# Every second unit of an up-projection by seven products of quarters, in a one-core float32 decoder layer

## Chip, cores and metric

One Trainium2 chip, one of its cores. The metric is the device time of one execution in microseconds (us); lower is better.

## What is computed

One step of a hybrid decoder layer on 2048 prompt rows and 32 sample rows, width 1024, all in float32. The part that the change touches is the channel mixer behind the first layer norm:

```python
def conv_glu_ffn(x, conv_state, w_up, conv_w, conv_b, w_down):      # x: rows x 1024
    L = x.shape[1]
    a, g = jnp.split(x @ w_up, 2, axis=-1)                          # w_up: 1024 x 5632
    ext = jnp.concatenate([conv_state.astype(a.dtype), a], axis=1)
    conv = conv_b
    for j in range(CONV_W):                                         # 3 taps
        conv = conv + ext[:, j:j + L] * conv_w[j]
    h = jax.nn.gelu(conv) * g
    return h @ w_down, ext[:, -(CONV_W - 1):]                       # w_down: 2816 x 1024
```

Before it stand the input projection, a state-space branch, window attention and their merge; behind it a residual sum and a second layer norm.

## The kernel before

The 2048 prompt rows are taken in four blocks of 512; the 32 sample rows ride with the second block, whose tiles are 544 columns wide and whose products run as 256 and 288 columns. In a block the stages follow one another: input projection, state-space branch and attention beside the gates, merge, first layer norm, up-projection and down-projection.

**A product of float32 matrices is three.** Each operand is split into a high and a low part (`x1h`, `x1l` of the activations, `wh`, `wl` of the weights), and high by high, high by low and low by high are summed in PSUM (`ws_unit`, the matmuls of L262). A weight tile `wr` (128 x 1024, six buffers) comes by DMA from the SP queue; `split_to` (L220) makes `wh` on ACT by a copy and `wl` on DVE by a subtraction, or on POOL (`G`) when the tile's place in the program's list `order` leaves 2 on division by 3. `wh` and `wl` have four buffers each. `W.get(key)` takes the next tile of the list, issues loads up to three tiles further on and splits up to two tiles further on; `W.ahead()` does one more split. So a weight is split in program order among the other work of ACT and DVE, a little ahead of its matmuls.

**A unit of the up-projection** is 128 of the 2816 hidden channels: tile `ua` gives the convolution's half, `ug` the gate's half, each 24 matmuls of 512 columns (8 slices of 128 input channels, 3 products). `ffn_tail` then works on one tile after another: ACT copies PSUM to `ae`, ACT makes the first tap `cv`, DVE adds two taps, ACT squares into `cq`, DVE multiplies, ACT takes the tanh, DVE finishes the gelu; `ffn_gate` multiplies by the gate from PSUM on DVE, and `split` makes `hh` on ACT and `hl` on DVE for the down-projection. The split of a weight stands between the taps and the gelu (`meanwhile`).

**Groups.** The 22 units stand in two groups of 12 and 10 (`GROUPS`). Behind each group comes its part of the down-projection: two halves `h` of 512 output columns, `nu` weight tiles `dn` in each, 24 matmuls of 512 columns a tile; `dn_evict` adds the result to the rows `z` (tiles `xr`) on DVE.

The program is not reordered: the instructions of each engine stand in the order in which the code writes them, and `bg.tick()` (one per half unit or `dn` tile) is where background steps of other stages are written in: the layer norm's scaling of the rows on POOL (`x1_rows`), the transposes of the next block's input (`x_split`) and so on.

## Time and profile before

| | |
|---|---|
| median of 3 runs | 2846.28 us (2841.29 to 2846.91) |
| profiled execution | 2843.99 us |
| its span, first to last instruction | 2842.2 us |
| PE (matmuls) busy | 2811.4 us, 99% of the span, 15180 matmuls |
| PEld (weight loads) busy | 2392.7 us, 84% |
| DVE, ACT, POOL busy | 1698.5 us (60%), 1162.1 us (41%), 1005.9 us (35%) |
| DMA | 304.25 MB, mean 107 GB/s |
| mean granted TensorE clock | 0.997 of 2.4 GHz |

The profiled execution lies 2.3 us under the median; 1.8 us of it lie outside the span. PE is TensorE's matmuls and PEld its weight loads, which overlap them; DVE is VectorE, ACT ScalarE, POOL GpSimd, SP the engine that issues most DMAs. A busy PE is not a PE at its peak, since the records of successive matmuls overlap.

### The profile page before, as it was taken

How to read it: one execution, taken by the hardware profiler on the slowest of the kernel's cores; microseconds unless marked ns; L12 is line 12 of the kernel's file. 1: busy time of each engine (PE TensorE's matmuls, PEld its weight loads, DVE VectorE, ACT ScalarE, POOL GpSimd, SP SyncE). 2: the span in 40 equal slices, each digit the busy share in tenths (PEclk: the TensorE clock that was granted, in tenths of full speed). 3: DMA queues.
4: the chain of work that ended last, by engine and by line, in shares of the span. 5: the costliest groups of instructions: out<-in, count | busy, mean ns of one | idle time of the engine just before them, and what ended most of it. 6: DMA issues, size and time to landing. Idle time of an engine off the chain costs nothing.

```text
span 2842.2 us, 39299 instructions
## 1 busy us (share of the span) xinstructions
PE 2811.4 (99%) x15180; PEld 2392.7 (84%) x15180; DVE 1698.5 (60%) x2673; ACT 1162.1 (41%) x2039; POOL 1005.9 (35%) x1070
## 2 busy tenths in 40 slices
PE   9999999999999999999999999999999999999998
PEld 8887888888999989989978878888888887888887
DVE  6984676254586467634647735762545854674355
ACT  4535354243335426423424442542433453344241
POOL 1764244121445413512207731351124661252122
PEclk9999999999999999999999999999999999999999
DMA  5423233334622432223345324223245433233232
GB/s 155 154 78 119 81 90 105 93 97 135 180 71 70 132 107 80 89 69 106 106 119 180 99 79 134 82 97 104 87 136 155 118 101 126 82 97 111 82 98 76
DMA packets 414494, 304.25 MB, mean 107 GB/s; under 512 B 51147, under 2 KB 350498, under 8 KB 414290
## 3 DMA queue, kind: packets, MB, share of 16 engines
q1 hardware_dynamic: 411490, 293.77, 34.5%
q0 software_dynamic: 2816, 7.96, 0.8%
q8 instruction: 119, 1.95, 0.3%
q14 instruction: 69, 0.57, 0.1%
HBM read 285.30 MB, written 17.39 MB: 106 GB/s over the span
## 4 chain that ended last, share of the span: by engine, by line
PE 91%; DVE 4%; POOL 2%; issue 1%; ACT 1%; DMA 0%; DVEq 0%; POOLq 0%; SPq 0%; ACTq 0%
PE ps L262 58%; PE ps L266 9%; PE ps L268 8%; PE ps L267 8%; PE ps L318 3%; PE ps L989 1%; POOL m L121 1%; PE ps L799 1%; DVE wl L121 1%; DVE t L121 1%; PE ps L274 1%; DVE m L121 0%; POOL ht L121 0%; PE ps L939 0%; DVE scr L121 0%
## 5 line engine op out<-in xcount | busy, mean ns | idle before, releaser
L121 POOL TENSOR_TENSOR wl<-wr,wh 128x1024 fp32r<-128x1024 f32 x136 | 338.0, 2485 | 899.0 <-ACT wh L113 806.6
L113 ACT ACTIVATE wh<-wr 128x1024 fp32r<-128x1024 f32 (+1 forms) x449 | 470.3, 1050 | 261.0 <-PE ps L268 250.2
L262 PE MATMUL ps<-x1l,wh 128*128 128x512 f32 (+2 forms) x1856 | 569.1, 342 | 0.0
L262 PE MATMUL ps<-x1h,wl 128*128 128x512 f32 (+2 forms) x1856 | 567.6, 341 | 0.0
L262 PE MATMUL ps<-x1h,wh 128*128 128x512 f32 (+2 forms) x1856 | 567.5, 341 | 0.0
L121 DVE TENSOR_TENSOR wl<-wr,wh 128x1024 fp32r<-128x1024 f32 (+1 forms) x313 | 407.8, 1306 | 201.1 <-ACT wh L113 199.9
L262 PEld LDWEIGHTS ps<-x1h,wh 128*128 128x128 f32 x1856 | 325.5, 188 | 42.9 <-issue 0.8
L262 PEld LDWEIGHTS ps<-x1l,wh 128*128 128x128 f32 x1856 | 325.7, 188 | 42.1 <-DVE x1l L121 0.3
L262 PEld LDWEIGHTS ps<-x1h,wl 128*128 128x128 f32 x1856 | 325.6, 188 | 41.0
L262 PE MATMUL ps<-xh,wh 128*128 128x512 f32 (+1 forms) x880 | 285.8, 357 | 5.5 <-ACT yk L113 1.4
L262 PE MATMUL ps<-xh,wl 128*128 128x512 f32 (+1 forms) x880 | 281.0, 352 | 5.1 <-POOL wl L121 2.5
L118 DVE SCALAR_TENSOR_TENSOR cv<-ae,pc,cv 128x512 f32<-128x512 f32 x176 | 145.4, 826 | 227.1 <-ACT cv L115 224.0
L262 PE MATMUL ps<-xl,wh 128*128 128x512 f32 (+1 forms) x880 | 280.5, 351 | 0.0
L266 PE MATMUL ps<-wh,hh 128*128 128x512 f32 x704 | 279.9, 398 | 0.0
L268 PE MATMUL ps<-wh,hl 128*128 128x512 f32 x704 | 277.9, 395 | 0.0
L267 PE MATMUL ps<-wl,hh 128*128 128x512 f32 x704 | 277.0, 394 | 0.0
L1654 POOL COPY cc<-ae 128x2 f32<-128x2 f32 x88 | 19.6, 223 | 492.2 <-ACT ae L113 491.4
L262 PEld LDWEIGHTS ps<-xh,wh 128*128 128x128 f32 x880 | 156.2, 189 | 30.2 <-issue 2.4
L262 PEld LDWEIGHTS ps<-xh,wl 128*128 128x128 f32 x880 | 156.3, 189 | 29.7 <-DVE wl L121 3.9
L262 PEld LDWEIGHTS ps<-xl,wh 128*128 128x128 f32 x880 | 156.7, 189 | 20.3
L266 PEld LDWEIGHTS ps<-wh,hh 128*128 128x128 f32 x704 | 132.6, 188 | 34.6 <-issue 5.0
L268 PEld LDWEIGHTS ps<-wh,hl 128*128 128x128 f32 x704 | 132.2, 188 | 30.9
(357 smaller groups left out, 4889.6 us busy)
## 6 DMA issues: line engine op xcount, KB each, us to landing
wr<-in_w_up SPq DMA_DIRECT2D x176, 512.0 KB
wr<-in_w_down SPq DMA_DIRECT2D x88, 512.0 KB
wr<-in_w_in SPq DMA_DIRECT2D x87, 512.0 KB
wr<-in_w_glu SPq DMA_DIRECT2D x64, 256.0 KB
wr<-in_w_o SPq DMA_DIRECT2D x32, 512.0 KB
wr<-in_w_in SPq DMA_DIRECT2D x34, 256.0 KB
xin<-in_x_prompt SPq DMA_DIRECT2D x32, 256.0 KB
wr<-in_w_attn_br SPq DMA_DIRECT2D x32, 256.0 KB
```

The lines of the kernel that those rows point to most:

```text
L113: A.activation(out, in_, AF.Copy, scale=scale, **kw)
L118: eng.scalar_tensor_tensor(out, a, s, b, op0=op0, op1=op1, **kw)
L121: eng.tensor_tensor(out, a, b, op=op)
L262: T.matmul(ps[:, :n], w[:, k, :], x[k][:, c0:c0 + n], start=(i == 0), stop=(i == len(ops) - 1))
L266: T.matmul(ps[:m], ah, wh, start=first, stop=False)
L267: T.matmul(ps[:m], ah, wl, start=False, stop=False)
L268: T.matmul(ps[:m], al, wh, start=False, stop=last)
L274: T.matmul(ps[r:r + 32], a, w, start=(k < 4), stop=(k >= n - 4))
L318: T.transpose(out, in_, ident[:k, :k])
L799: T.matmul(xv[:, a, r, :], C.t[n][:, a_ * 128:(a_ + 1) * 128], C.uv[:, a_, :], start=True, stop=True)
L989: T.matmul(B.ops[qb][r, :], vt[:, qb + kt, r], pt[kt], start=(kt == 0), stop=(kt == 1))
L1654: G.tensor_copy(cc[:, :, f], ae[:, 512:514])
```

## The change

For two square halves of rows and of channels, a product of 2 x 2 quarters can be made of seven products of sums of quarters in place of eight. The change takes the tokens of a block in two halves (`hn` = 256, or 272 in the second block) and the 1024 input channels in two halves; the two column halves are a unit's `a` and `g`. In blocks two to four, every second unit from unit 6 on (`F0`; units 6, 8, ..., 20) is made in this way by `seven(f)`: 7 products of 4 slices x 3 = 12 matmuls of `hn` columns, 84 in place of 48 of 512. The following odd unit stays as it was, and `two_units` writes both together, in the order `sc` (products 1 and 5), `sa` (2 and 6), `sb` (3 and 7), `ua` of the odd unit, `sd` (product 4), `ug` of the odd unit.

- **Sums of weights** are made once, in block one: `weight_sums`, one of three steps at each tick, loads four quarters of w_up (256 KB each), makes four sums on DVE, splits two of them, and writes 1.5 MB to DRAM; 8 times. Later `sc` and `sa` load a quarter and a sum (256 KB each) into a `wr` tile and split it on ACT and DVE, never on POOL; `sb` loads its high and low parts (512 KB each) straight into `wh` and `wl`; `sd` is half a tile.
- **Sums of activations** are made per block by `x1_sums` (12 background steps on DVE and ACT in the first group and its down-projection), from the whole-precision copies `x1f`, which now stay until then.
- **The results** are put together by `seven`: ACT copies products 1 and 5 to `us`; DVE adds 2 and 6, then 3 and 7, into `ae`, then runs the same taps and gelu, and makes the gate's half in `gt`.
- **Groups** are now four, of 6, 6, 4 and 6 units, The up-projection meets the down-projection four times a block, and the rows `z` are added to twice as often. `x1_rows` and `x_split` stand at closer ticks. In the last group of the last block all three `dn` tiles of the second half are held and run tile by tile (before: the last four of five). One small instruction in the very last layer norm goes from POOL to DVE.

The diff, cut to its core:

```diff
-GROUPS = ((0, 12), (12, 22))
+GROUPS = ((0, 6), (6, 12), (12, 16), (16, 22))
+LG = len(GROUPS) - 1
+F0 = 6
...
+    def weight_sums():
...
+                    t[i, j] = S("ws")
+                    SP.dma_start(k4(t[i, j][:, 0:512]), quarter(f, i, j))
+            yield
+            tt(t[1, 1], t[1, 0], t[1, 1], OP.add)
+            tt(t[1, 0], t[0, 0], t[1, 0], OP.subtract)
+            tt(t[0, 0], t[1, 1], t[0, 0], OP.subtract)
+            tt(t[0, 1], t[0, 1], t[0, 0], OP.subtract)
+            yield
+            hi = [S("wsh", dt=F32R) for _ in range(2)]
+            lo = [S("wsl", dt=F32R) for _ in range(2)]
+            for h, l, s in zip(hi, lo, (t[0, 1], t[1, 0])):
+                act(h, s)
+                tt(l, s, h.bitcast(F32), OP.subtract)
+            def out(f=f, s1=t[1, 1], s2=t[0, 0], hi=hi, lo=lo):
+                SP.dma_start(sums["s1", f], s1)
+                SP.dma_start(sums["s2", f], s2)
+                for n, x in (("hi", hi), ("lo", lo)):
+                    for i in range(2):
+                        SP.dma_start(sums[n, f][:, i * 512:(i + 1) * 512], x[i].bitcast(F32))
+            bg.add(1, out)
+            del t, hi, lo, out
+            yield
...
+        if k == "sa":
+            return lambda t: [(k4(t[:, 0:512]), quarter(key[1], 0, 1)), (t[:, 512:1024], sums["s2", key[1]])]
+        if k == "sc":
+            return lambda t: [(k4(t[:, 0:512]), quarter(key[1], 0, 0)), (t[:, 512:1024], sums["s1", key[1]])]
+        if k == "sd":
+            return lambda t: [(k4(t[:, 0:512]), quarter(key[1], 1, 1))]
...
+            dn = [("dn", g, h, i) for h in range(2) for i in range((f1 - f0) // 2)]
+            if b and f0 >= F0:
+                for f in range(f0, f1, 2):
+                    order += [("sc", f), ("sa", f), ("sb", f), ("ua", f + 1), ("sd", f), ("ug", f + 1)]
+                order += dn
+            else:
+                for f in range(f0, f1):
+                    order += [("ua", f), ("ug", f)]
+                order += dn
...
+                key = order[self.dmas]
+                if key[0] == "sb":
+                    two = [wp.tile([128, 1024], F32R, name=uid(n_), tag=n_, bufs=4) for n_ in ("wh", "wl")]
+                    for t, n_ in zip(two, ("hi", "lo")):
+                        SP.dma_start(t.bitcast(F32), sums[n_, key[1]])
+                    self.ready[self.dmas] = tuple(two)
+                    self.dmas += 1
+                    continue
...
         def split_to(self, n, eng=None):
             while self.splits < min(n, len(order)):
+                if self.splits in self.ready:
+                    self.splits += 1
+                    continue
                 t = self.raw.pop(self.splits)
+                c = 512 if order[self.splits][0] == "sd" else 1024
                 hi = wp.tile([128, 1024], F32R, name=uid("wh"), tag="wh", bufs=4)
                 lo = wp.tile([128, 1024], F32R, name=uid("wl"), tag="wl", bufs=4)
-                act(hi, t)
-                e = eng or (G if self.splits % 3 == 2 and self.splits > 24 and order[self.splits][0] != "u" else V)
-                tt(lo, t, hi.bitcast(F32), OP.subtract, eng=e)
+                act(hi[:, 0:c], t[:, 0:c])
+                e = eng or (G if self.splits % 3 == 2 and self.splits > 24
+                            and order[self.splits][0] not in ("u", "sa", "sc", "sd") else V)
+                tt(lo[:, 0:c], t[:, 0:c], hi[:, 0:c].bitcast(F32), OP.subtract, eng=e)
...
-            bg.add(6 + 3 * i, lambda i=i: x1_rows(i))
...
+        def x1_sums():
+            lo_, hi_ = slice(0, hn), slice(hn, n)
+            for k in range(4):
+                t12, t34 = S("t12", 544), S("t34", 544)
+                tt(t12[:, lo_], x1f[k][:, hi_], x1f[k][:, lo_], OP.subtract)
+                tt(t12[:, hi_], x1f[k + 4][:, hi_], t12[:, lo_], OP.subtract)
+                yield
+                tt(t34[:, lo_], x1f[k + 4][:, hi_], x1f[k][:, hi_], OP.subtract)
+                tt(t34[:, hi_], x1f[k + 4][:, lo_], t12[:, hi_], OP.subtract)
+                del x1f[k], x1f[k + 4]
+                th[0, k], tl[0, k] = split(B, t12, None, "t")
+                yield
+                th[1, k], tl[1, k] = split(B, t34, None, "t")
+                del t12, t34
+                yield
+        if B.b:
+            x1s = x1_sums()
+            for i in range(12):
+                bg.add(5 + i, lambda: next(x1s, None))
...
                 act(ae[:, 2 + c0:2 + c0 + c], pa[i][:, 0:c])
+            conv(f, ae, pa[1][:, 256:288] if B.sp else None)
+            meanwhile()
...
+        def product(o, w, part, x):
+            hi, lo = (k4(t[:, part * 512:part * 512 + 512]) for t in w)
+            ws_unit(hi, lo, 4, *x, [(0, hn)], [o])
...
+            w = W.get(("sc", f))
+            _, p1, p5 = banks()
+            product(p1, w, 0, quarters(0, 0))
+            product(p5, w, 1, row_sums(1))
+            u, gt, ae = S("us", 544), S("gt", 544), S("ae", 546)
+            G.tensor_copy(ae[:, 0:2], cc[:, :, f])
+            act(u[:, 0:hn], p1)
+            act(u[:, hn:n], p5)
+            del p1, p5, _
+            yield
+            w = W.get(("sa", f))
+            both, p2, p6 = banks()
+            product(p2, w, 0, quarters(1, 0))
+            product(p6, w, 1, row_sums(2))
+            add(ae[:, 2:2 + n], u[:, 0:hn], both, p2, p6)
+            del both, p2, p6
+            yield
+            w = W.get(("sb", f))
+            _, p3, p7 = banks()
+            product(p3, w, 0, quarters(1, 1))
+            product(p7, w, 1, row_sums(3))
+            c12 = ae[:, 2 + hn:2 + n]
+            tt(u[:, 0:hn], c12, p7, OP.add)
+            tt(c12, c12, p3, OP.add)
+            tt(c12, c12, u[:, hn:n], OP.add)
+            del p3, p7, _
+            conv(f, ae, ae[:, 514:546])
+            c_ = fst.c
+            del ae, c12
             q = S("cq", 544)
             act(q[:, 0:n], c_[:, 0:n], AF.Square)
+            yield
             stt(q[:, 0:n], q[:, 0:n], 1.0 / GELU_A, c_[:, 0:n], OP.add, OP.mult)
             act(q[:, 0:n], q[:, 0:n], AF.Tanh, scale=GELU_S * GELU_A)
+            yield
+            p4 = P()[:, 0:hn]
+            product(p4, W.get(("sd", f)), 0, row_sums(4))
             stt(c_[:, 0:n], q[:, 0:n], 1.0, c_[:, 0:n], OP.add, OP.mult)
-            fst.c = c_
+            tt(gt[:, hn:n], u[:, 0:hn], u[:, hn:n], OP.add)
+            tt(gt[:, 0:hn], u[:, 0:hn], p4, OP.add)
+            del p4
+            stt(c_[:, 0:n], c_[:, 0:n], 0.5, gt[:, 0:n], OP.mult, OP.mult)
+            hh[f], hl[f] = split(B, c_, None, "h", hs.get(f))
+            yield
+        def two_units(f):
+            t = seven(f)
+            next(t)
+            next(t)
+            bg.tick()
+            next(t)
+            w = [x.rearrange("p (k m) -> p k m", k=8) for x in W.get(("ua", f + 1))]
+            pa = ws_unit(*w, 8, x1h, x1l, cols)
+            next(t)
+            bg.tick()
+            next(t)
+            bg.tick()
+            ffn_tail(f + 1, pa, lambda: None)
+            w = [x.rearrange("p (k m) -> p k m", k=8) for x in W.get(("ug", f + 1))]
+            pg = ws_unit(*w, 8, x1h, x1l, cols)
+            hh[f + 1], hl[f + 1] = ffn_gate(f + 1, pg, W.ahead)
+            bg.tick()
...
+                if B.b == 0:
+                    bg.steps = weight_sums()
+            quartered = B.b and f0 >= F0
+            for f in range(f0, f1, 2) if quartered else ():
+                two_units(f)
+            for f in () if quartered else range(f0 or 2, f1):
...
-                        bg.add(2 + k, lambda k=k: x_split(nxt, k))
+                        bg.add(2 + k // 2, lambda k=k: x_split(nxt, k))
```

On DVE, in the third block's second group of units, the program before has, for one unit f and the start of the next (`ps` is PSUM, `xr` the rows, the other names are those above):

```order
L121 TENSOR_TENSOR hl_18771<-cv_18723,hh_18770 128x512
L118 SCALAR_TENSOR_TENSOR cv_18803<-ae_18799,pc,cv_18803 128x512 x2
L121 TENSOR_TENSOR wl_18810<-wr_18764,wh_18809 128x1024
L118 SCALAR_TENSOR_TENSOR cq_18813<-cq_18813,cv_18803 128x512
L118 SCALAR_TENSOR_TENSOR cv_18803<-cq_18813,cv_18803 128x512
L118 SCALAR_TENSOR_TENSOR cv_18803<-cv_18803,ps_18818 128x512
L121 TENSOR_TENSOR hl_18851<-cv_18803,hh_18850 128x512
```

The change has, on DVE in the same block, for units 6 and 7, from the split of unit 8's `sc` to behind the split of unit 8's `sa` (`wl_18379` and `wl_18420`):

```order
L126 TENSOR_TENSOR wl_18379<-wr_18340,wh_18378 128x1024
L123 SCALAR_TENSOR_TENSOR cv_18334<-cq_18338,cv_18334 128x512
L126 TENSOR_TENSOR gt_18262<-us_18261 128x256
L126 TENSOR_TENSOR gt_18262<-us_18261,ps_18374 128x256
L123 SCALAR_TENSOR_TENSOR cv_18334<-cv_18334,gt_18262 128x512
L126 TENSOR_TENSOR hl_18399<-cv_18334,hh_18398 128x512
L123 SCALAR_TENSOR_TENSOR cv_18406<-ae_18402,pc,cv_18406 128x512 x2
L123 SCALAR_TENSOR_TENSOR cq_18410<-cq_18410,cv_18406 128x512
L123 SCALAR_TENSOR_TENSOR cv_18406<-cq_18410,cv_18406 128x512
L126 TENSOR_TENSOR wl_18420<-wr_18375,wh_18419 128x1024
L123 SCALAR_TENSOR_TENSOR cv_18406<-cv_18406,ps_18423 128x512
L126 TENSOR_TENSOR hl_18452<-cv_18406,hh_18451 128x512
```

Before, one unit's taps and gelu stand between two splits; now the end of unit 6 and the taps and gelu of unit 7 stand between the splits of `sc` and `sa`.

On ACT, before, for one unit of that group:

```order
L113 ACTIVATE hh_18770<-cv_18723 128x512
L113 ACTIVATE ae_18799<-ps_18774 128x512
L115 ACTIVATE cv_18803<-ae_18799,pc 128x512
L113 ACTIVATE wh_18809<-wr_18764 128x1024
L115 ACTIVATE cq_18813<-cv_18803 128x512
L115 ACTIVATE cq_18813<-cq_18813 128x512
L113 ACTIVATE wh_18846<-wr_18807 128x1024
L113 ACTIVATE hh_18850<-cv_18803 128x512
```

With the change, on ACT, for units 6 and 7, from unit 6's first tap to unit 7's `hh` (`wh_18343` is unit 7's `ug`, `wh_18378` unit 8's `sc`, `wh_18419` unit 8's `sa`):

```order
L120 ACTIVATE cv_18334<-ae_18263,pc 128x512
L120 ACTIVATE cq_18338<-cv_18334 128x512
L118 ACTIVATE wh_18343<-wr_18299 128x1024
L120 ACTIVATE cq_18338<-cq_18338 128x512
L118 ACTIVATE wh_18378<-wr_18340 128x1024
L118 ACTIVATE hh_18398<-cv_18334 128x512
L118 ACTIVATE ae_18402<-ps_18347 128x512
L120 ACTIVATE cv_18406<-ae_18402,pc 128x512
L120 ACTIVATE cq_18410<-cv_18406 128x512
L120 ACTIVATE cq_18410<-cq_18410 128x512
L118 ACTIVATE wh_18419<-wr_18375 128x1024
L118 ACTIVATE hh_18451<-cv_18406 128x512
```

Unit 7's copy out of PSUM, `ae_18402`, now stands behind unit 6's last step, `hh_18398`, and the split of unit 8's `sa` behind unit 7's tanh.

## Rows read from the trace of the kernel before

**Rows 1.** The page: the chain that ended last, shares of the span by engine.

```profile
PE 91%; DVE 4%; POOL 2%; issue 1%; ACT 1%; DMA 0%; DVEq 0%; POOLq 0%; SPq 0%; ACTq 0%
```

**Rows 2.** Waits, engine PE: who was waited for; us in total, times, longest.

```profile
PE ps L858 <- POOL ht L121: 3.0, 1, 3.0
PE ps L262 <- POOL wl L121: 2.5, 1, 2.5
```

**Rows 3.** Windows: us, busy us (xinstructions) of PE, PEld, DVE, ACT, POOL, PEclk, DMA, GB/s.

```profile
2000.00:2100.00 100.00, 100.00 (x434) 81.20 (x433) 58.48 (x67) 47.00 (x64) 21.12 (x23) 1.00 0.37 118
...
1300.00:1420.00 120.00, 120.00 (x960) 120.00 (x959) 72.73 (x102) 56.79 (x106) 29.74 (x46) 1.00 0.34 106
```

**Rows 4.** Timeline, PE: start us, us, instruction; 256-column matmuls, 45 rows with both ends.

```profile
1797.92 0.28 PE L262 MATMUL ps<-x1h,wl 128*128 128x256 f32 x1
...
1803.15 0.28 PE L262 MATMUL ps<-x1l,wh 128*128 128x256 f32 x1
```

**Rows 5.** Lines by form, DVE, 1992 to 2103: xcount | busy us, mean ns | idle before.

```profile
L121 DVE TENSOR_TENSOR wl<-wr,wh 128x1024 fp32r<-128x1024 f32 x13 | 15.9, 1220 | 0.0
L118 DVE SCALAR_TENSOR_TENSOR cv<-ae,pc,cv 128x512 f32<-128x512 f32 x20 | 15.0, 752 | 36.6 <-ACT cv L115 36.2
...
L118 DVE SCALAR_TENSOR_TENSOR cv<-cq,cv 128x512 f32<-128x512 f32 x9 | 6.2, 693 | 6.3 <-ACT cq L115 6.3
```

**Rows 6.** Lines by form, ACT, 1992 to 2103.

```profile
L113 ACT ACTIVATE wh<-wr 128x1024 fp32r<-128x1024 f32 x19 | 19.9, 1045 | 0.0
L115 ACT ACTIVATE cv<-ae,pc 128x512 f32<-128x512 f32 x10 | 8.2, 816 | 0.9
L115 ACT ACTIVATE cq<-cv 128x512 f32<-128x512 f32 x10 | 6.3, 633 | 6.6 <-DVE cv L118 6.6
L113 ACT ACTIVATE ae<-ps 128x512 f32<-128x512 f32 x10 | 6.0, 600 | 37.8 <-PE ps L262 37.8
```

**Rows 7.** Lines by form, DVE, whole span: adds of 256 columns from PSUM.

```profile
L121 DVE TENSOR_TENSOR m<-ps,tber 128x256 f32<-128x256 f32 x16 | 6.7, 417 | 0.1
```

**Rows 8.** Timeline, 2008 to 2021: one unit's chain on ACT and DVE, beside POOL.

```profile
2009.42 0.60 ACT L113 ACTIVATE ae<-ps 128x512 f32<-128x512 f32 x1 [3.43 <-PE ps L262]
...
2011.96 2.81 POOL L121 TENSOR_TENSOR wl<-wr,wh 128x1024 fp32r<-128x1024 f32 x1 [1.62 <-ACT wh L113]
...
2013.20 2.12 DVE L118 SCALAR_TENSOR_TENSOR cq<-cq,cv 128x512 f32<-128x512 f32 x1 [0.70 <-ACT cq L115]
...
2016.02 0.69 DVE L118 SCALAR_TENSOR_TENSOR cv<-cq,cv 128x512 f32<-128x512 f32 x1 [0.70 <-ACT cq L115]
...
2020.53 0.60 ACT L113 ACTIVATE ae<-ps 128x512 f32<-128x512 f32 x1 [2.36 <-PE ps L262]
```

**Rows 9.** Timeline, PE: the longest wait.

```profile
184.93 0.49 PE L858 MATMUL ps<-cw,ht 128*128 128x128 f32 x2 [2.98 <-POOL ht L121]
```

**Rows 10.** Windows behind and around waits of PE.

```profile
187.10:190.40 3.30, 3.30 (x14) 3.00 (x13) 1.70 (x9) 2.48 (x8) 1.15 (x2) 0.50 0.04 12
190.50:194.00 3.50, 3.50 (x17) 2.88 (x16) 1.52 (x4) 0.00 (x0) 3.25 (x3) 1.00 0.22 64
278.00:282.60 4.60, 2.77 (x11) 1.74 (x10) 2.17 (x6) 1.28 (x5) 0.00 (x0) 1.00 0.58 164
282.70:286.00 3.30, 3.30 (x9) 2.60 (x8) 0.45 (x1) 0.00 (x0) 0.00 (x0) 0.50 0.00 0
1519.00:1524.00 5.00, 2.52 (x11) 1.73 (x11) 4.91 (x5) 3.44 (x5) 4.92 (x5) 1.00 0.07 26
```

**Rows 11.** Windows: first block's second group; third block's start of the up-projection.

```profile
553.00:665.00 112.00, 112.00 (x489) 90.78 (x488) 65.20 (x84) 51.17 (x72) 21.52 (x29) 1.00 0.37 117
...
1790.00:1857.00 67.00, 67.00 (x393) 59.04 (x392) 50.37 (x68) 35.05 (x52) 28.55 (x28) 1.00 0.35 102
```

**Rows 12.** Windows: the kernel's start, the highest DMA rate asked for.

```profile
20.00:30.00 10.00, 10.00 (x51) 9.59 (x51) 4.12 (x8) 7.25 (x15) 0.00 (x0) 1.00 1.12 291
```

More of the change, by code (lines that the diff above doesn't have):

```diff
@@ L51, in __init__ @@
     def __init__(self):
+        self.steps = iter(())
         self.now = 0
@@ L72, in tick @@
             x[4]()
+        if not draining:
+            next(self.steps, None)
     def drain(self):
         while self.todo:
-            self.tick()
+            self.tick(True)
 @with_exitstack
@@ L132, in u_cols, with quarter, k4 @@
                            w[r0:r0 + 128 * kk, c0:c0 + m].rearrange("(k p) m -> p k m", p=128))]
+    sums = {}
+    for f in range(F0, NF, 2):
+        for n in ("s1", "s2"):
+            sums[n, f] = dram.tile([128, 512], F32, name=f"sum_{n}_{f}")
+        for n in ("hi", "lo"):
+            sums[n, f] = dram.tile([128, 1024], F32, name=f"sum_{n}_{f}")
+    def quarter(f, i, j):
+        c0 = i * DFF + f * 128
+        return w_up[512 * j:512 * j + 512, c0:c0 + 128].rearrange("(k p) m -> p k m", p=128)
+    def k4(t):
+        return t.rearrange("p (k m) -> p k m", k=4)
+    def weight_sums():
+        for f in range(F0, NF, 2):
+            t = {}
+            for i in range(2):
+                for j in range(2):
+                    t[i, j] = S("ws")
[15 more added lines that the diff above has]
+                for n, x in (("hi", hi), ("lo", lo)):
+                    for i in range(2):
+                        SP.dma_start(sums[n, f][:, i * 512:(i + 1) * 512], x[i].bitcast(F32))
+            bg.add(1, out)
+            del t, hi, lo, out
+            yield
     def unit_src(key):
         k = key[0]
+        if k == "sa":
[4 more added lines that the diff above has]
+            return lambda t: [(k4(t[:, 0:512]), quarter(key[1], 1, 1))]
         if k == "u":
@@ L1621, in body @@
         acc3 = wo_second(3)
+        if B.b:
+            x1f.update({k: S("x1f", 544) for k in range(8)})
         upper, whole, lower = x1_evict(0)
@@ L1644, in body, with quarters, row_sums @@
         for i in range(B.nt):
-            bg.add(6 + 3 * i, lambda i=i: x1_rows(i))
+            bg.add(4 + 2 * i, lambda i=i: x1_rows(i))
         fst = Blk()
+        hn = n // 2
+        th, tl = {}, {}
+        def x1_sums():
[13 more added lines that the diff above has]
+                yield
+        if B.b:
+            x1s = x1_sums()
+            for i in range(12):
+                bg.add(5 + i, lambda: next(x1s, None))
+        def quarters(i, j):
+            return [[t[4 * i + k][:, j * hn:j * hn + hn] for k in range(4)] for t in (x1h, x1l)]
+        def row_sums(i):
+            r, j = divmod(i - 1, 2)
+            return [[t[r, k][:, j * hn:j * hn + hn] for k in range(4)] for t in (th, tl)]
         def ffn_tail(f, pa, meanwhile):
@@ L1738, in body @@
                 hs.update(zip(range(f0, f1), wide(f1 - f0)))
-            if g == 1 and nxt is not None and nxt.sp:
+            if g == LG and nxt is not None and nxt.sp:
                 steps = sample_consts(nxt)
@@ L1753, in body @@
                 bg.tick()
-            if g == 1:
-                x1h.clear()
-                x1l.clear()
+            if g == LG:
+                for x in (x1h, x1l, th, tl):
+                    x.clear()
                 if nxt is not None:
@@ L1799, in body @@
                                          + [W.kept])
-                outer = 4 if B.last and g == 1 and h == 1 else 0
+                outer = nu if B.last and g == LG and h == 1 else 0
                 for i in range(nu - outer):
@@ L1808, in body @@
                 if outer:
-                    four = [get(nu - 4 + i, i) for i in range(4)]
+                    four = [get(nu - outer + i, i) for i in range(outer)]
                     for t in range(B.nt):
-                        for i in range(4):
-                            dn_mm(t, nu - 4 + i, four[i])
+                        for i in range(outer):
+                            dn_mm(t, nu - outer + i, four[i])
                         dn_evict(t)
```

50 lines of the change are left out of this document (34 added, 16 removed).

## Prediction, made before the change was run

> **What bounds the kernel now.** I read the chain that ended last first: 91% of it is PE [rows 1]. Then PE's waits: the longest of the whole run is 3.0 us, the next 2.5 us [rows 2], so PE is fed almost everywhere and time goes by its columns. Then the windows, for the price of a column: 434 matmuls of 512 columns in 100 us, 0.230 us each; in the second block 960 in 120 us, alternately 256 and 288 columns, 0.125 us each of 272 on average [rows 3]. From the first to the last of 45 matmuls of 256 columns it is 5.23 us, so 0.119 us each [rows 4]. Last, the work beside PE. DVE is busy 58 us in 100 and ACT 47 [rows 3], which looks like room. But the reader should see its shape: a unit's taps and gelu are one chain that changes between ACT and DVE at every step, from 2009.42 to 2016.71, 7.3 us long, and comes again after 11.1 us, the 48 matmuls of a unit [rows 8]. It is hidden because it has a whole unit's time.
>
> **The matmuls.** Removed are 16 units x 48 = 768 of 512 columns (176.9 us at 0.230) and, in the second block, 8 x 96 = 768 of 272 on average (96.0 us). Added are 16 x 84 = 1344 of 256 columns (159.9 us at 0.119) and 8 x 84 = 672 of 272 (84.0 us). That is 272.9 against 243.9: **29 us less**, if PE never waits more than before.
>
> **A rule that speaks against the matmuls.** PEld is busy all of the 120 us of the second block's window and 81 of 100 us in the third's [rows 3], and the change adds 480 weight loads. Still 256-column matmuls, one load each, follow at 0.119 us in that window and at [rows 4].
> The Trainium skill, Perfetto Trace Analysis, section Identifying the Most-Contended Engine, would have headroom on TensorE judged by the busy share of LDWEIGHTS and not by that of matmuls; by it there is none left for more loads, and the 29 us would be zero or a loss, so that the sum below would be 102 us or more. The trace does not agree: at a full share the matmuls still cost what their columns cost.
>
> **The new order of a pair.** PE's order is `sc`, `sa`, `sb`, `ua`, `sd`, `ug`, then the next pair. The split of the next pair's `sa` is issued by the `get` of `ug`, and that stands behind `ffn_tail` of the odd unit; this in turn stands, on ACT and on DVE, behind the last step of the even unit (the order shown with the change). So between the end of `sb`'s products and the next `sa` there is one serial chain of two units. Its steps, with the durations of before: three DVE adds of 256 columns at 0.42 [rows 7]; first tap on ACT 0.82 [rows 6]; two taps on DVE 1.50 [rows 5]; square 0.63; split of `ug`, 1.05 on ACT [rows 6] and 1.22 on DVE [rows 5]; multiply 0.69; tanh 0.63; split of the next `sc`, 1.05 and 1.22; then on DVE 0.69 to finish the gelu, two adds for the gate 0.84, the gate 0.69; `hh` on ACT 0.63. That is 12.92 us. Then the odd unit: `ae` 0.60 [rows 6], tap 0.82, taps 1.50, square 0.63, multiply 0.69, tanh 0.63, split of `sa` 1.05 and 1.22: 7.14 us. In all 20.1 us. (I price all DVE steps of 512 columns at the 0.69 of the gelu's last step [rows 5], ACT's at the 0.63 of the square. Hops cost little: DVE waited 0.70 us for the tanh of 0.63 [rows 8].)
>
> In that time PE has `ua` 24 x 0.230 = 5.5, `sd` 12 x 0.119 = 1.4, `ug` 5.5, the next `sc` 24 x 0.119 = 2.9: 15.3 us. The low part is needed only at `sa`'s third matmul, 0.24 us later. So PE waits 20.1 - 15.3 - 0.2 = **about 4.5 us at the next pair's `sa`**. The next pair's chain starts again at the end of its `sb`, so the delay is never caught up inside a group: a pair takes 21.0 + 4.5 = 25.5 us where two units took 22.1.
>
> There are 5 such places in a block, 15 in all (pairs but the last of each group). Which engine splits `ug` goes by the tile's place in the list. In 10 of the 15 it is DVE: 10 x 4.5 = 45 us. The second block is among these: its steps are longer, but so are its matmuls. In 5 it is POOL, and the chain is shorter by DVE's 1.22 and by what the tanh no longer waits, 1.9 in all; POOL's 2.81 us [rows 8] ends close to where `ug` starts. 5 x 2.6 = 13 us.
>
> **Ends of groups.** After a last pair PE has `dn` tile 0, 24 x 0.23 = 5.5 us, where `sc` stood: 18.0 us, until tile 1, whose split stands at the chain's end. That waits 1.9 us with DVE, about 3 with POOL, and in the groups of four units about 4, because tile 1 needs the odd unit's `hh` and `hl` as well; where POOL took `ug`, 0 to 2. Over 9 ends I take 2.2 each: **20 us**.
>
> **The clock.** After the longest wait of before, 2.98 us [rows 9], the granted clock stands at 0.50 (1.2 GHz) from 187.1 to 190.4 us and is back at 1.00 from 190.5; it does so again behind 4.6 us of which PE was idle 1.8; around the wait of 2.48 us at 1520 it stays at 1.00 [rows 10]. In the second half-clock window 9 matmuls took 3.3 us, 0.37 each. 3.4 us at half rate cost 1.7 us of PE's work, and behind a wait at `sa` they fall on `sa` and `sb`, which lie ahead of the next chain. 14 of the 24 waits would be longer than 2.9 us (10 at `sa`, 4 at ends): 14 x 1.7 = **24 us**. The bounds are 0, and 41 if all 24 do it.
>
> **What I cost at nothing.** The sums of weights in the first block: 8 x 2.5 MB in 24 ticks of 5.5 us is 150 GB/s beside 117 [rows 11], under the 291 shown at the start [rows 12]; on DVE 8 x (6 x 0.69) = 33 us fit into the 47 idle of 112 [rows 11] and the down-projections. Without that cover it is a few us: 0 to 8. `x1_sums` adds some 12 us to DVE where it is 75% busy, 50 of 67 us [rows 11], while POOL's `x1_rows` stand closer, and a DVE step beside POOL can take 2.12 instead of 0.69 [rows 8]; a unit's chain has 3.8 us to spare: 0 to 5 in each of three blocks. The weights of `sb` are asked for when the `ua` before is done, with 12 us until use, 1 MB being 4 us at 291 GB/s. The doubled adds to `z`, 64 x 0.69 on DVE, lie beside 24 matmuls a tile. The instruction moved from POOL in the last norm gains under 1 us.
>
> **The sum.** -29 + 45 + 13 + 20 + 24 = +73 us on the profiled execution's 2844: **2917 us**, 2.5% slower. (The median of the runs lies 2.3 us above that execution.)
>
> **Rivals.** *All hidden.* If the two chains run side by side, or the splits come earlier than the order says, PE stays the bound and the time is 2844 - 29 = 2815. For it: the mean shares of DVE and ACT, and PE's lack of waits now. Against it: DVE and ACT would have to do the 20.1 us in 15.3, and no step in it can pass another on its engine. It decides at a chain of 15.5 us. Chance 0.08. *Waits and gain cancel.* The chain is some 3 us shorter than I sum (a split done while its engine idles anyway), and no clock is lost: -29 + 15 x 1.5 + 9 x 0.7 = 0, 2844. Chance 0.03. *Weight loads bind.* If each of 84 took the 188 ns that a load is recorded with (81.2 us over 433 [rows 3]), an even unit would take 15.8 us where it took 11.1: 24 x 4.7 = 113, 2957; against it [rows 4]. Chance 0.02. *DVE is late in other places too* (first block, first groups): the forecast and 8 + 15 us more, 2940. Chance 0.07. That the change does not do what it says is excluded by the order: the 2016 matmuls of 256 and 272 columns stand there. The forecast has 0.80.
>
> **Numbers.** The range goes down to the forecast without the clock's 24 us and with 1.5 us less at each of 24 places, -60: 2857; and up to all bounds together, 17 of the clock, 8 and 15, some 40: 2957. It leaves out the hidden case and the tie, 0.11, and some of the forecast's own error. Three runs of before lie 0.2% apart, so that is what I call no change. Faster: the hidden case, 0.08. Within 0.2%: 0.03. Slower: 0.89.
>
> **What would show it.** Right: PE waits of 4 to 5 us on DVE's `wl` at the line of `ws_unit`, ten or more of them, in the up-projection of blocks two to four; DVE's step just before each wait is the gelu of an odd unit; 256-column matmuls at 0.119 us; dips of the granted clock behind the waits; the first block as long as before. Wrong: PE's waits stay under 1 us there, or they name DMA or weight loads.

## The result, and the profile after

The changed kernel takes 2967.43 us (median of four runs, 2966.75 to 2968.68) against 2844.03 us before: a ratio of 1.0434, 95% interval 1.0416 to 1.0452, **4.3% slower**. The forecast was 2917 us with a range up to 2957. The direction is right, the loss is 123 us where 73 were forecast, and the time lies outside the range. The profiled execution's span grew from 2842.2 to 2965.0 us.

First the page: PE's share fell from 99% to 96%, so PE is idle for 117 us of the span where it was for 31. But its busy time grew too, by 36 us, although its matmuls should take 29 us less, and the page does not say why. (Columns: busy us, share of the span, instructions.)

```profile
PE 2847.8 (96%) x15660; PEld 2432.2 (82%) x15660; DVE 1913.1 (65%) x3061; ACT 1187.9 (40%) x2119; POOL 961.6 (32%) x1050
```

Next PE's waits (PE's line and whom it waited for: us in total, times, longest us). Before, the longest two were 3.0 and 2.5 us and each came once [rows 2].

```profile
PE ps L337 <- ACT wh L118: 44.9, 16, 3.8
PE ps L342 <- DVE wl L126: 13.5, 10, 4.1
PE ps L337 <- DVE wl L126: 12.7, 20, 1.7
PE ps L337 <- POOL wl L126: 7.4, 9, 3.1
PE ps L342 <- POOL wl L126: 5.8, 3, 1.9
PE ps L341 <- ACT wh L118: 5.3, 7, 1.0
```

L337 is the matmul of `ws_unit`, L341 to L343 are those of the down-projection. One such wait, in the third block, read in the timeline of PE, DVE and ACT (start us, duration us, instruction, in brackets the idle time before it and who ended it; the rows stand in order within each engine):

```profile
1980.13 0.40 PE L337 MATMUL ps<-x1h,wh 128*128 128x512 f32 x1
...
1999.17 0.58 PE L337 MATMUL ps<-x1h,wh 128*128 128x256 f32 x1 [3.51 <-ACT wh L118]
...
2000.43 0.58 PE L337 MATMUL ps<-x1h,wl 128*128 128x256 f32 x1 [0.47 <-DVE wl L126]
```

```profile
1980.33 0.42 DVE L126 TENSOR_TENSOR us<-ae,ps 128x256 f32<-128x256 f32 x1 [1.96 <-PE ps L337]
...
1991.80 0.69 DVE L123 SCALAR_TENSOR_TENSOR cv<-cv,gt 128x512 f32<-128x512 f32 x1
...
1999.15 1.23 DVE L126 TENSOR_TENSOR wl<-wr,wh 128x1024 fp32r<-128x1024 f32 x1 [0.25 <-ACT wh L118]
```

```profile
1992.52 0.63 ACT L118 ACTIVATE hh<-cv 128x512 fp32r<-128x512 f32 x1 [3.28 <-DVE cv L123]
1993.06 0.58 ACT L118 ACTIVATE ae<-ps 128x512 f32<-128x512 f32 x1
...
1997.54 0.63 ACT L120 ACTIVATE cq<-cq 128x512 f32<-128x512 f32 x1 [0.76 <-DVE cq L123]
1998.08 1.04 ACT L118 ACTIVATE wh<-wr 128x1024 fp32r<-128x1024 f32 x1
```

At 1980.13 `ua` follows on `sb` and the first of the three adds starts at 1980.33. The even unit's `hh` ends at 1993.1, the odd unit's tail follows at once, and only behind its tanh stands the split of the next `sa`, at 1998.08. PE needs its high part at 1995.7 and gets it at 1999.17; the low part at 2000.43. From the first add, at the end of `sb`, to the matmul on the low part it is 20.1 us. It is 20.1 us at all seven places of this kind in blocks three and four, and 21.5 us at the three in the second block, whose steps are longer.

Last the windows over that group (us; busy us and instructions of PE, PEld, DVE, ACT, POOL; PEclk, DMA, GB/s), then a wait at `sa` and the stretches behind it:

```profile
1943.20:2020.60 77.40, 69.24 (x397) 61.95 (x396) 43.74 (x62) 27.73 (x42) 1.55 (x10) 0.91 0.40 123
```

```profile
1967.00:1970.70 3.70, 0.21 (x2) 0.01 (x1) 2.06 (x3) 2.21 (x3) 0.00 (x0) 1.00 0.60 179
1970.90:1977.80 6.90, 6.24 (x29) 5.94 (x30) 4.26 (x6) 2.64 (x5) 0.00 (x0) 0.51 0.00 0
1977.90:1982.00 4.10, 4.10 (x29) 3.74 (x29) 1.74 (x4) 0.24 (x1) 0.20 (x2) 1.00 0.00 0
```

Three pairs took 77.4 us, where the same six units take 66.6 with nothing quartered (e_groups, below). DVE was busy 43.7 of these 77.4 us, 57%, so it is not short of time. And the clock is at 0.5 (1.2 GHz) for 6.8 us behind one wait, where behind the longest wait of before it was 3.4 [rows 10].

**Where the 123 us are.** I took the start-to-start time of all neighbouring matmuls of the two traces and set against each the median of the same two shapes at full clock. The sums differ as follows; the forecast's terms stand beside them. (Another way of taking the medians moves the lines on the matmuls' lengths by up to 3 us.)

| | measured, us | forecast, us |
|---|---|---|
| matmuls at their full-clock medians | -30.6 | -29 |
| waits at `sa`, odd unit split by DVE (10) | +41 | +45 |
| waits at `ug` and `sa`, POOL (5) | +16 | +13 |
| ends of groups | +15 | +20 |
| other waits of PE, mostly first groups and first block | +13 | 0 (bounds 0 to 23) |
| longer matmuls in half-clock stretches | +48 | +24 |
| longer matmuls next to a wait, at full clock | +10 | 0 |
| 512-column matmuls 1.2 ns longer everywhere | +9 | 0 |
| sum | +122 | +73 |

### The profile page after: what moved, and what is told of

It is laid out like the page before. It is cut to its first block, busy times and chain, and to the rows that moved or that the text cites. A ratio compares the mean times of both kernels' runs of the same rounds, so it can differ in the third digit from the quotient of the medians.

```text
span 2965.0 us, 41201 instructions
## 1 busy us (share of the span) xinstructions
PE 2847.8 (96%) x15660; PEld 2432.2 (82%) x15660; DVE 1913.1 (65%) x3061; ACT 1187.9 (40%) x2119; POOL 961.6 (32%) x1050
## 5 line engine op out<-in xcount | busy, mean ns | idle before, releaser
L126 DVE TENSOR_TENSOR wl<-wr,wh 128x1024 fp32r<-128x1024 f32 (+1 forms) x353 | 453.0, 1287 | 211.6 <-ACT wh L118 208.1
L118 ACT ACTIVATE wh<-wr 128x1024 fp32r<-128x1024 f32 (+1 forms) x473 | 479.8, 1027 | 187.5 <-PE ps L343 148.8
L126 POOL TENSOR_TENSOR wl<-wr,wh 128x1024 fp32r<-128x1024 f32 x120 | 297.1, 2476 | 788.2 <-ACT wh L118 757.5
L337 PE MATMUL ps<-x1h,wh 128*128 128x256 f32 (+3 forms) x1632 | 506.6, 338 | 43.8 <-ACT wh L118 43.8
L337 PE MATMUL ps<-x1h,wl 128*128 128x256 f32 (+3 forms) x1632 | 506.9, 338 | 14.8 <-DVE wl L126 10.5
L337 PE MATMUL ps<-x1l,wh 128*128 128x256 f32 (+3 forms) x1632 | 503.5, 336 | 0.0
L337 PEld LDWEIGHTS ps<-x1h,wh 128*128 128x128 f32 x1632 | 297.0, 192 | 79.1 <-ACT wh L118 46.9
L337 PEld LDWEIGHTS ps<-x1h,wl 128*128 128x128 f32 x1632 | 297.1, 192 | 54.3 <-DVE wl L126 15.9
L337 PEld LDWEIGHTS ps<-x1l,wh 128*128 128x128 f32 x1632 | 297.5, 192 | 31.3
L337 PE MATMUL ps<-xh,wh 128*128 128x512 f32 (+1 forms) x880 | 287.9, 359 | 5.4 <-ACT yk L118 1.4
L341 PE MATMUL ps<-wh,hh 128*128 128x512 f32 x704 | 284.4, 404 | 5.9 <-ACT wh L118 4.7
L337 PE MATMUL ps<-xh,wl 128*128 128x512 f32 (+1 forms) x880 | 283.4, 355 | 5.4 <-POOL wl L126 3.1
L343 PE MATMUL ps<-wh,hl 128*128 128x512 f32 x704 | 282.0, 401 | 1.6 <-DVE hl L126 1.6
L337 PE MATMUL ps<-xl,wh 128*128 128x512 f32 (+1 forms) x880 | 282.1, 353 | 0.0
L337 PEld LDWEIGHTS ps<-xh,wl 128*128 128x128 f32 x880 | 157.3, 190 | 30.9 <-DVE wl L126 3.6
L337 PEld LDWEIGHTS ps<-xh,wh 128*128 128x128 f32 x880 | 157.4, 190 | 30.6 <-issue 2.4
L342 PEld LDWEIGHTS ps<-wl,hh 128*128 128x128 f32 x704 | 135.0, 192 | 55.0 <-DVE wl L126 17.6
L337 PEld LDWEIGHTS ps<-xl,wh 128*128 128x128 f32 x880 | 157.4, 190 | 21.2
L341 PEld LDWEIGHTS ps<-wh,hh 128*128 128x128 f32 x704 | 134.7, 191 | 46.7 <-ACT wh L118 8.2
```

Of the source, the lines that this page charges most:

```text
L118: A.activation(out, in_, AF.Copy, scale=scale, **kw)
L126: eng.tensor_tensor(out, a, b, op=op)
L337: T.matmul(ps[:, :n], w[:, k, :], x[k][:, c0:c0 + n], start=(i == 0), stop=(i == len(ops) - 1))
L341: T.matmul(ps[:m], ah, wh, start=first, stop=False)
L342: T.matmul(ps[:m], ah, wl, start=False, stop=False)
L343: T.matmul(ps[:m], al, wh, start=False, stop=last)
```

## The experiments

The theory (A): the split of the next `sa` stands behind two units' chain on in-order engines; that makes the waits in the pairs, and the waits make the half clock. All ratios are to the kernel before, which ran on the same chips.

**1. The groups alone (e_groups).** Nothing is quartered; no sums of weights, none of x1.

```diff
-F0 = 6
+F0 = 22
-            if B.b:
+            if 0:
                 fk = lambda k: x1f[k][:, sl]
-        if B.b:
+        if 0:
             x1f.update({k: S("x1f", 544) for k in range(8)})
-        if B.b:
+        if 0:
             x1s = x1_sums()
```

Expected:

> The change with no unit by seven products, no weight sums and no sums of x1 (F0 = 22): what is left is four groups instead of two and the background steps placed closer. Theory A (the waits in the quartered pairs and the clock that falls after them make the loss; groups alone cost little): within 12 us of the kernel before, 2840 to 2856 us, PE waits inside the up-projection units under 8 us in sum. Rival B (the regrouping itself, its extra evictions and group ends with their waits for weight splits, costs a large part): 2875 us or more.

Measured: 2848.66 us, ratio 1.0018 (1.0009 to 1.0028), and no wait of PE in any up-projection. Four groups, the doubled adds and the closer steps cost about 5 us. Rival B falls. The window over the six units that the change makes in 77.4 us:

```profile
1896.70:1963.30 66.60, 66.60 (x289) 54.05 (x289) 36.49 (x42) 29.49 (x40) 11.14 (x14) 1.00 0.27 86
```

**2. The groups and the sums (e_sums).** Weight sums are made and stored, x1's sums are made, neither is used: units as before.

```diff
-            if b and f0 >= F0:
+            if 0:
-            quartered = B.b and f0 >= F0
+            quartered = False
```

Expected:

> The change with its groups, its weight sums in block one (made and stored, then not used) and its sums of x1 in the first group of blocks two to four, but every unit computed as before the change. Theory A: block one keeps its +6.6 us and the first groups of blocks two to four their late weight splits of the first down-projection unit (8.0 us of waits and the clock after some of them): 2855 to 2875 us, so that some 95 us of the loss are in the quartered pairs alone. Rival B (sums and groups cost most): 2900 us or more. Rival C (the first-group waits come from the quartered pairs behind them): 2850 us or less.

Measured: 2866.95 us, ratio 1.0086 (1.0071 to 1.0101). The sums cost 18 us over e_groups, in the first block and at the first down-projection of the others, with the waits of the changed kernel (longest 4.1 us). So some 100 of the 123 us are in the quartered pairs, and that is net of what their matmuls save.

How some 12 us of DVE work become a wait of 4.1 us is seen in the changed kernel's timeline of the second block's first group, DVE, POOL and then PE:

```profile
1156.15 1.80 DVE L123 SCALAR_TENSOR_TENSOR cq<-cq,cv 128x544 f32<-128x544 f32 x1
1158.67 0.73 DVE L123 SCALAR_TENSOR_TENSOR cv<-cq,cv 128x544 f32<-128x544 f32 x1 [0.72 <-ACT cq L120]
...
1168.42 2.46 DVE L123 SCALAR_TENSOR_TENSOR cv<-ex,pc,cv 128x32 f32<-128x32 f32 x2
1170.81 1.21 DVE L126 TENSOR_TENSOR wl<-wr,wh 128x1024 fp32r<-128x1024 f32 x1
```

```profile
1155.12 2.25 POOL L126 TENSOR_TENSOR xr<-xr,b1t 128x512 f32<-128x512 f32 x1
1159.67 2.41 POOL L126 TENSOR_TENSOR wl<-wr,wh 128x1024 fp32r<-128x1024 f32 x1 [2.30 <-ACT wh L118]
...
1168.03 1.59 POOL L126 TENSOR_TENSOR xr<-xr,b1t 128x512 f32<-128x512 f32 x1
1169.58 1.26 POOL L126 TENSOR_TENSOR xr<-xr,g1t 128x512 f32<-128x512 f32 x1
```

```profile
1172.07 0.64 PE L342 MATMUL ps<-wl,hh 128*128 128x512 f32 x1 [4.10 <-DVE wl L126]
```

The split that PE waits for takes DVE 1.21 us; it is late because of what stands ahead of it. And what stands there is slow while POOL works on `x1_rows`: the gelu's first step of 544 columns took 1.80 us beside POOL, the next one, while POOL was idle, 0.73; taps of 32 columns took 1.23 each. The rest of this trace agrees. The gelu's first step of 512 columns took 0.68 to 0.69 us in all 50 cases with no POOL work beside it, and 1.77 to 2.12 in the nine that POOL work covered. A tap of 32 columns took 0.25 in 34 cases without POOL work. The step that takes the gate from PSUM took 0.67 to 0.69 with or without it.

**3. PE kept at work through the wait (e_warm).** The wait for the split stays; small products fill it.

```diff
             both, p2, p6 = banks()
+            if f not in [f_ for f_, _ in GROUPS]:
+                for i in range(14 if W.pos % 3 == 2 else 30):
+                    T.matmul(p2[:, 0:128], ident, mask[:, 0, :], start=True, stop=True)
```

Expected:

> The changed kernel with small products of 128 columns (ident by mask, some 0.105 us each, result overwritten) put on PE just before the products of `sa` in every quartered pair but a group's first: 30 of them (3.15 us) where DVE splits the weights of the odd unit's second half, 14 (1.5 us) where POOL does. The wait for the split of `sa` itself stays as long as it was, PE is only kept at work through most of it. Theory A (the half clock of 6.83 us follows a wait of PE, and costs some 3.4 us each time): half-clock time falls from 120 us by 60 to 75 us, time 2930 to 2942 us. Rival D (the half clock follows from the pattern of short products, or of all waits, the small ones too): half-clock time within 15 us of that of the change, time 2960 to 2970 us; if the products delay what is behind them, up to 3000 us.

Measured: 2960.03 us, ratio 1.0416 (1.0399 to 1.0434). Half-clock time fell as theory A has it, from 122 to 47 us; the time did not. The reason is in the trace: 30 products are 60 matmuls and ran for 6.9 us, in a wait of 4.

```profile
1991.57 6.86 PE L1831 MATMUL ps<-mask,ident 128*128 128x128 f32 x60
1998.19 0.36 PE L337 MATMUL ps<-x1h,wh 128*128 128x256 f32 x1
```

So the run decides on the clock's cause and not on its price, and I had mispriced my own filler by two. It was repeated with half.

**4. Half as many (e_warm2).** As above with 7 and 15.

Expected:

> As e_warm with half as many small products: 15 and 7. In e_warm one of them took 0.221 us, not 0.105, so that 30 of them ran for 6.6 us in a wait of some 4 us: half-clock time fell by 75 us, and the products ran some 31 us past the waits. Here they take 3.3 and 1.5 us, inside the waits. Theory A (half clock follows a wait of PE and is paid beside it): half-clock time 45 to 60 us, time 2927 to 2940 us. Rival D (what was gained by the clock in e_warm was lost in another way than by the products' length): 2955 us or more.

Measured: 2941.53 us, ratio 1.0346 (1.0332 to 1.0361), just past the 2940 of theory A, and half-clock time 52 us. 26 us came back although no split came earlier (from the first add to the low part it is 20.1 us here too). The filler took the place of the wait (39 us for 40), 31 us of half-clock loss went away by the matmuls' lengths, and some 5 us came in, about half of it at matmuls next to the two short waits that are left at each place. Behind such a place in the third block the clock is now full:

```profile
1965.70:1972.60 6.90, 6.08 (x49) 5.87 (x50) 4.94 (x6) 2.65 (x6) 0.00 (x0) 1.00 0.00 0
```

The half clock is caused by PE's idle time in the waits and is paid beside them.

**5. The pair in another order (e_order).** The same instructions on the same engines. Shortened, in the order in which ACT and DVE get them; the change has them as on the - lines:

```diff
+            w = [x.rearrange("p (k m) -> p k m", k=8) for x in W.get(("ua", f + 1))]
+            pa = ws_unit(*w, 8, x1h, x1l, cols)
             conv(f, ae, ae[:, 514:546])
...
+            w = W.get(("sd", f))
+            p4 = P()[:, 0:hn]
+            product(p4, w, 0, row_sums(4))
+            q0 = gelu(c0_)
...
+            conv(f + 1, ae, pa[1][:, 256:288] if B.sp else None)
+            w = [x.rearrange("p (k m) -> p k m", k=8) for x in W.get(("ug", f + 1))]
+            pg = ws_unit(*w, 8, x1h, x1l, cols)
...
             stt(c0_[:, 0:n], c0_[:, 0:n], 0.5, gt[:, 0:n], OP.mult, OP.mult)
+            q1 = gelu(c1_)
             hh[f], hl[f] = split(B, c0_, None, "h", hs.get(f))
...
-            ffn_tail(f + 1, pa, lambda: None)
-            w = [x.rearrange("p (k m) -> p k m", k=8) for x in W.get(("ug", f + 1))]
-            pg = ws_unit(*w, 8, x1h, x1l, cols)
-            hh[f + 1], hl[f + 1] = ffn_gate(f + 1, pg, W.ahead)
+            hh[f + 1], hl[f + 1] = ffn_gate(f + 1, pg, ahead)
```

(`gelu` is the square and the first DVE step; `ahead` splits up to the next `ua`, in a group's last pair as far as before.)

Expected:

> The changed kernel with the same instructions on the same engines, but the pair's work written in another order: the weight splits of the next pair's `sc` and `sa` stand on ACT and DVE ahead of the odd unit's gelu tail instead of behind it, that of the next `ua` stands before the split of the last gated unit, and the tails of the even and the odd unit are interleaved. No work is taken out. Theory A (a chain of splits behind the odd unit's tail, in order on ACT and DVE, makes the 3.5 us waits, and they make most of the half clock): the waits of PE for weights in the pairs fall from 73 us to 20 us or less, the half clock with them, 2830 to 2875 us. Rival E (ACT and DVE have too much work in the quartered stretches, order is no matter; the waits show up elsewhere): 2935 us or more.

Measured: 2841.77 us, ratio 0.9994 (0.9985 to 1.0004). **126 us came back by order alone**, and no wait of PE is left in a quartered group. The window over the same group, and ACT at the place where the next `sa` is split:

```profile
1902.50:1965.70 63.20, 63.20 (x398) 56.82 (x397) 46.13 (x65) 31.41 (x46) 9.15 (x12) 1.00 0.49 155
```

```profile
1939.14 0.82 ACT L120 ACTIVATE cv<-ae,pc 128x512 f32<-128x512 f32 x1
1939.86 1.04 ACT L118 ACTIVATE wh<-wr 128x1024 fp32r<-128x1024 f32 x1
1941.56 0.63 ACT L120 ACTIVATE cq<-cv 128x512 f32<-128x512 f32 x1 [0.66 <-DVE cv L123]
1943.75 0.63 ACT L118 ACTIVATE hh<-cv 128x512 fp32r<-128x512 f32 x1 [1.56 <-DVE cv L123]
```

The split (1939.86) now stands between the odd unit's first tap and its square, 7 us ahead of its use. DVE is busy 73% here and nobody waits; in the change it was busy 57% and PE waited. Rival E falls. PEld is busy 56.8 of the 63.2 us, 90%, and PE has no gap: the rival on weight loads falls too. The Trainium skill, Perfetto Trace Analysis, section Identifying the Most-Contended Engine, judges TensorE's headroom by the share of peak arithmetic (MFU) and by the busy share of LDWEIGHTS. For the second of these the trace does not agree: a column costs 0.45 to 0.46 ns here at 90% as it did at 81 and at 100% [rows 3].

**6. Only one edit of it (e_simple).** The `get` of `ug` and its products ahead of the odd unit's tail.

```diff
-            ffn_tail(f + 1, pa, lambda: None)
             w = [x.rearrange("p (k m) -> p k m", k=8) for x in W.get(("ug", f + 1))]
             pg = ws_unit(*w, 8, x1h, x1l, cols)
+            ffn_tail(f + 1, pa, lambda: None)
```

Expected:

> The changed kernel with one edit of e_order alone: the odd unit's second half (`ug`: its get, by which the next `sa` is split, and its products) is written ahead of the odd unit's gelu tail. Theory A, if the split of `sa` behind the tail is the whole of it: waits in the pairs 25 us or less, 2860 us or less. Theory A in its wider form (a whole pair's work on ACT and DVE, in order, is a loop of some 24 us against 21.1 us on PE, and the wait only moves to another split): waits in the pairs 45 to 75 us, at `sa` or at `ua`, 2900 to 2955 us. Rival (moving it delays the tail and so the hidden rows of the group): 2967 us or more.

Measured: 2914.31 us, ratio 1.0251 (1.0237 to 1.0266). 53 us come back and the wait moves, as the wider form says: from `sa` to `ua`, here in the third block.

```profile
1959.23 0.28 PE L337 MATMUL ps<-th,wl 128*128 128x256 f32 x1
1961.07 0.50 PE L337 MATMUL ps<-x1h,wh 128*128 128x512 f32 x1 [1.56 <-ACT wh L118]
1961.40 0.40 PE L337 MATMUL ps<-x1l,wh 128*128 128x512 f32 x1
```

Waits in the quartered groups are 46 us in sum, against 73. The longest single one, 4.7 us, is at a group's end, where PE waits for the odd unit's `hh`: that is what the third rival named, at one place. So this move alone is not enough, and the interleaved order of e_order is. That no place of the splits would do without interleaving is argued from the sum of a pair's steps (some 24 us against 21.1 on PE) and not shown.

**7. e_order without the early split of `ua` (e_noearly).**

```diff
-            hh[f + 1], hl[f + 1] = ffn_gate(f + 1, pg, ahead)
+            hh[f + 1], hl[f + 1] = ffn_gate(f + 1, pg, W.ahead)
```

Expected:

> e_order without one of its parts: the split of the next pair's `ua` stands where the change has it, at the `get` of `sa`, and not ahead of the last gate's split. The interleaved tails and the early splits of `sc` and `sa` stay. Theory A (what matters is that the split of `sa` does not stand behind the odd unit's tail): 2838 to 2850 us, waits in the pairs under 10 us. Rival H (the early `ua` is needed because DVE's and ACT's lists are full at that place): waits at `ua` of 1 us or more in most pairs, 2860 us or more.

Measured: 2841.09 us, ratio 0.9990 (0.9980 to 0.9999), no wait in a quartered group. That part of e_order was not needed; rival H falls.

**8. The sums alone moved (e_late).** The pairs stay in the change's order.

```diff
-                bg.add(5 + i, lambda: next(x1s, None))
+                bg.add(10 + (i + 1) // 2, lambda: next(x1s, None))
-                if B.b == 0:
-                    bg.steps = weight_sums()
+            if g == 1 and B.b == 0:
+                bg.steps = weight_sums()
```

Expected:

> The changed kernel, its pairs in the order of the change, with the sums alone moved: weight sums from block one's second group on, sums of x1 on the ticks of the first group's down-projection. e_best against e_order gave 13.4 us for this move. Theory A (the sums' cost is a term of its own, waits at the first groups, and adds to that of the pairs): 2950 to 2958 us, waits in the pairs as in the change, 72 to 76 us. Rival G (in the changed order the sums' delay is taken up by the waits in the pairs behind it, or sums that stand later lengthen these): 2963 us or more.

Measured: 2947.22 us, ratio 1.0370 (1.0350 to 1.0391), single runs from 2943 to 2955: 3 us under the expected range. Waits in the quartered groups are 74 us, against 73 in the change, so the two costs stand side by side and rival G falls. What was not expected is the clock. In the third block the waits at `sa` for ACT's `wh` are the same to 0.1 us, but the stretch at half clock behind each of the five is 3.4 us, where in the change it was 6.8 at four of them:

```profile
1957.19 0.39 PE L337 MATMUL ps<-x1h,wh 128*128 128x256 f32 x1 [3.43 <-ACT wh L118]
...
1958.45 0.48 PE L337 MATMUL ps<-x1h,wl 128*128 128x256 f32 x1 [0.75 <-DVE wl L126]
```

```profile
1958.60:1962.00 3.40, 3.40 (x17) 3.40 (x18) 1.91 (x3) 2.64 (x5) 0.00 (x0) 0.50 0.00 0
1962.10:1966.00 3.90, 3.90 (x34) 3.81 (x33) 1.87 (x4) 0.00 (x0) 0.00 (x0) 1.00 0.00 0
```

Of ten waits at `sa` of 4.0 to 4.5 us, nine had 6.8 us of half clock behind them in the changed kernel's profile, three in this one's. The loss by half-clock matmuls is 34 us here and 52 there. Those 18 us are more than the 10 that this profiled execution, of 2943 us, gained beyond the 13 of the same move in e_best over e_order. How long the clock is low is not fixed by the kernel either: its four executions had a mean granted clock of 0.987, 0.987, 0.981 and 0.979 and took 2943, 2943, 2951 and 2955 us, so two of them lie in the expected range. Only the first of the four was read wait by wait.

**9. Both together (e_best).** The pairs of e_order and the sums of e_late.

Expected:

> The reordered pair of e_order, and the sums moved to where DVE has room: the weight sums begin with block one's second group instead of behind its first units, and the sums of x1 stand on the ticks of the first group's down-projection (two a tick) instead of those of its last units. e_sums against e_groups gave 18 us for the sums: +5.9 in block one, +6.3, +4.8 and +1.6 in the first groups of blocks two to four. Theory A (those waits come from DVE work that stands ahead of a weight split, not from the sums' amount or their transfers): the waits at the first down-projection units (2.0+0.7, 4.1, 1.4 and 2.5 us) go, 2822 to 2832 us. Rival F (the amount decides: the sums only make something else late): 2838 us or more.

Measured: 2828.34 us, ratio 0.9950 (0.9936 to 0.9964): **0.5% faster than the kernel before**, 139 us faster than the change as it was made. The largest waits left are mostly those of before; at the first down-projections, where the change had 4.1 us, 1.6 is the most:

```profile
PE ps L337 <- POOL wl L126: 3.1, 1, 3.1
PE ps L933 <- POOL ht L126: 2.9, 1, 2.9
PE ps L342 <- DVE wl L126: 2.5, 3, 1.6
```

By the same comparison of matmuls, its span of 2825.5 us against 2842.2 is -30.6 for the matmuls, +3 of waits, +2 of half clock and +9 for the longer 512-column matmuls. The move shifts the sums' transfers together with their DVE work; that the DVE work is what made the waits rests on the timeline under e_sums, and no run parts the two.

## Why the prediction was right in its direction and wrong in its size

- **The matmuls: right.** -30.6 us measured for -29, and it is the whole of what the change can give. The 256-column matmuls followed at 0.118 to 0.119 us everywhere.
- **The serial chain: right.** 20.1 us were summed, 20.1 are in the timeline of blocks three and four. The second block's 21.5 was foreseen as longer steps beside longer matmuls. Where POOL split `ug` the chain was 18.9 us, in the second block 20.3, for 18.2. The waits at `sa` are 41 us for 45 and 16 for 13; group ends 15 for 20. A detail was wrong: the wait was said to be for DVE's `wl`. It is for ACT's `wh` first (3.5 us), then for `wl` (0.5), since the high half of the split also stands behind the tanh. e_order shows that the order is the cause.
- **The clock: the step that failed most.** The sum put 14 waits at 1.7 us each, the price of the 3.4 us dip of before, which makes 24 us, and bounded the term by 41. 48 us came. Most waits at `sa` were followed by twice as long a stretch at half clock, and some ends of groups and POOL waits had one too. e_warm2 shows that the waits cause it. The two or three rows of before showed that a dip exists; they could not bound its length, and the upper bound should have allowed for that. The Trainium skill, TensorE: Matmul & The Clock Gate, section HAM oscillation — how this bites in real kernels, tells of a loop that waits for data at every tile and falls to the low clock each time. The trace agrees for the ten waits of 4.0 to 4.5 us at `sa`, each of which has a stretch at half clock behind it, and for three of the five shorter ones, of 2.2 to 2.5 us; in all the change has 122 us at half clock against 19 before (6 and 8 of them behind the last matmul). With 48 in its place the sum gives 2941 us, still inside the range: the rest of the miss is the terms put at nothing, in the next two points.
- **What was costed at nothing: about 18 us** (e_sums against e_groups), of the 23 that "DVE late elsewhere" named. It belonged in the sum: the group was seen to be 75% busy on DVE, to get 12 us more, and to run slower beside POOL. e_best shows that another place for the same work takes most of it away. It was given 0.07 as a rival, though it excludes nothing of the forecast; it came together with it. One sign of being right, "the first block as long as before", failed with it: the same early matmul of the second block starts at 790.03 us where it started at 783.55.
- **Not in the sum at all: some 19 us.** Matmuls next to a wait take longer, 10 us over the additional waits (in e_simple the next one starts 0.33 us behind that of 1961.07, where 0.23 is usual). And 512-column matmuls took about 1.2 ns more from start to start on average, 9 us in all; it is 1.0 to 1.6 ns in every kernel with quartered pairs, and 0.2 and 0.4 in e_groups and e_sums. It shows in the first block already, where nothing is quartered (from 553 to 660 us 232.1 ns on average, against 231.3 before); its cause stays open.
- **The rivals.** "All hidden" needed a chain of 15.5 us; in the order given it could not be, and e_best came within 13 us of its 2815, 9 of them the longer 512-column matmuls, once the two chains ran side by side. The mean shares of DVE and ACT did show the room; they could not show whether an order uses it.

The range ended at 2957 because the clock's bound and the sums' bounds were added, but with nothing for the starts and stops, and with the clock's bound from a single dip.

## What to carry to other kernels

When a change saves time on the bounding engine, write down for each weight split (or whatever feeds that engine) what stands ahead of it on its own in-order engine, and sum that chain against the time that the bounding engine has until use: here 20 us against 15, and the sum was right to 0.1 us in blocks three and four. If it does not fit, the order of issue is the first thing to change: the same instructions, interleaved, gave back 126 us. And repeated waits of 3 to 4 us are to be priced with the clock and the restart behind them: here 85 us of waits brought 58 us more, in e_simple 57 brought 34.

## What the runs showed of the hardware that was not expected

- The same wait is followed by different stretches at half clock. After waits at `sa` of 4.0 to 4.5 us the granted clock stood at 0.5 for 6.8 us nine times in ten in one kernel and three times in ten in another; the rest had 3.4. In the first of the two the stretch began between 1.9 us before and 0.8 us after the matmul that ended the wait for `wh`. Executions of the second differ too, with a mean granted clock from 0.979 to 0.987.
- Small products of f32 that fill a wait keep the clock: with PE at work through 3.3 of the 4 us, no stretch at half clock was left at any wait at `sa`.
- Each filler product, of 128 columns by an f32 operand, was two matmuls in the record and took 0.22 us. One of the two follows the other at 0.11 us, as the kernel's own 128-column matmuls do.
- A DVE step of 544 columns took 1.80 us while POOL worked on the rows of the layer norm, and a like step 0.73 without; a tap of 32 columns took 1.23 against 0.25. The DVE step that takes the gate from PSUM took the same with or without POOL work beside it.
